# The norm of the context's tokens for its second FFN is listed ahead of the latents' mixers of the first layer

## The chip, the cores and the metric

The kernel runs on one core of a Trainium2 chip. The metric is the device time of one execution in microseconds (us), the median of three runs. The core's engines are called PE (matrix products), DVE (element-wise work on 128 partitions), ACT (activations and copies), POOL (a second element-wise engine) and SP (which issues the DMAs here); each of them works through its own list of instructions, and an instruction waits for semaphores that others raise.

## What is computed

Two layers of a diffusion backbone run over 512 latent tokens `x` and 256 context tokens `ctx`, of width 1024 each. A layer is half an FFN, four mixers side by side (convolution, RG-LRU, RWKV-7, attention) between one input projection and one output projection, and half an FFN again. In the first layer the context has its own mixers and its own second FFN; the latents' attention, RG-LRU and RWKV take states from the context. In the second layer the context only feeds the latents' mixers. Cut to what matters:

```python
def rms_norm(x): return x * rsqrt(mean(x * x, -1) + EPS)
def modulate(x, shift, scale): return rms_norm(x) * (1 + scale) + shift
def swiglu(h, w13, w2):
    gate, up = split(h @ w13, 2); return (silu(gate) * up) @ w2
for l in range(2):
    x  = x  + 0.5 * g1  * swiglu(modulate(x,  sh1,  s1),  ffn1_w13[l], ffn1_w2[l])
    xc = xc + 0.5 * g1c * swiglu(modulate(xc, sh1c, s1c), ffn1_w13[l], ffn1_w2[l])
    u, uc = modulate(x, sh2, s2) @ w_in[l], modulate(xc, sh2c, s2c) @ w_in[l]
    ya..yd, yca..ycd = conv, lru, rwkv, attention of u (with states of uc) and of uc
    x = x + g2 * concat(ya..yd) @ w_out[l]
    if l == 0:
        xc = xc + g2c * concat(yca..ycd) @ w_out[l]
        xc = xc + 0.5 * g3c * swiglu(modulate(xc, sh3c, s3c), ffn2_w13[l], ffn2_w2[l])   # its modulate is what the change lists elsewhere
    x = x + 0.5 * g3 * swiglu(modulate(x, sh3, s3), ffn2_w13[l], ffn2_w2[l])
return rms_norm(x, final_norm)
```

## The kernel before

Activations lie transposed in the core's memory: eight tiles of 128 features by 512 (or 256) tokens for `x` (or `ctx`). The numbers are float32, and a product is made of three cheaper ones: `h` and a weight are each held as a high and a low part. For a weight tile there is a load from memory (`loadw`, L483, issued on SP), a cast to the high part on ACT (`splitw`, L496, `whi`), a subtraction for the low part on DVE or POOL (L500, `wlo`), and then `gemm` (L509): 16 matmuls with `whi` and 8 with `wlo` for 128 columns of output. There are three buffers for `raw`, two for `whi` and `wlo` each, and three banks for the results that are called `pg`.

A norm (`norm`, L460 and following) has two steps. `squares` is 8 squarings on ACT (L445, tile `nsq`, two buffers) and 8 additions on POOL and DVE (L448, L450, tile `nacc`), and then it yields. The second step sums over the features with one matmul against ones on PE (`colsum`, L406, into a `pg` bank), takes the root on ACT (L415) and the reciprocal on DVE (L416), and makes 8 tiles of `h`, each by a product on DVE (L471, tile `nt`), the high part on ACT (L472) and the low part on DVE (L473); then it yields again. The norm of `x` ahead of the mixers is done in two halves of 256 tokens; the norm of `ctx` in one.

What runs when: Python lists the instructions; a scheduler then orders each engine's list ahead of time, by a model of its own in which what is listed earlier has the higher priority and what is listed later fills idle time. So the place in the listing decides the place on an engine, and on the chip each engine keeps to the order it was given. In the first layer, `Net.run` lists the mixers of the latents, `mix(0, sx, ...)`, and behind them the rest of `ff`, a chain of generators with the norm and the second FFN of the context. The scheduler takes instructions of `ff` forward into the mixers wherever an engine has nothing else to do; this is called the filler below.

`mix` for the latents is, in order: the input projections (`winproj_c`, `winproj`: matmuls L509 of `h_6104`.. `h_6111` with `w_in`, each result read by ACT at L732, L734 or L805, L815), the depthwise convolution on DVE (`taps`, L841, tile `ac`), attention's values and keys (L914, L915 `vt`, L924) and gates (a gelu at L817 to L821, tile `gy`; L819 is its ACT function), the RG-LRU (L873 and following), the RWKV scan, and the output projection.

Of the kernel before, what the change touches and what calls it, by code (L numbers as in the profile page):

```python
# [133 lines left out]
def upto(g, blocks):  # L134

    for end in g:
        blocks -= end
        yield
        if not blocks:
            return  # L140


def some(g, n):

    for _ in g:
        for _ in range(n - 1):
            next(g, None)
        yield
# [31 lines left out]
class Net:  # L180
# [1149 lines left out]
    def run(self):  # L1330
# [3 lines left out]
        with self.hidden(sx) as f:  # L1334
            self.weights("left", 4, 3, 3)
            with self.pool("aw", "right") as ap:
# [10 lines left out]
                def feed():  # L1347
                    while True:
                        next(todo, None)
                        yield  # L1350
# [3 lines left out]
                def after():  # L1354
                    yield from self.norm(f.fp, hx.hs, 0, 1, sx)

                ff = self.ffn_groups(0, "ffn1_w13", "ffn1_w2", 0, sx, f, feed(), after())
# [29 lines left out]
        with self.hidden(sc) as f:  # L1387
            late = upto(a1, 1)
            ff = chain(self.norm(f.fp, f.hs, 0, 2, sc), self.ffn_groups(0, "ffn2_w13", "ffn2_w2", 2, sc, f, late))
            self.mix(0, sx, True, None, hx.hs)  # L1390
            hp = self.hold("fh", "right")
            fx = Unit(hs=self.htiles(hp, sx))
            with self.pool("wn", "right") as wp:
                done(self.norm(wp, fx.hs, 0, 2, sx, self.pM))
            done(chain(ff, late))
            f.hs = self.htiles(f.hp, sc)
            done(self.norm(f.fp, f.hs, 1, 0, sc))
            self.ffn(1, "ffn1_w13", "ffn1_w2", 0, sc, f)
        f = fx
        with self.pool("fw") as f.fp:  # L1400
            hs = self.htiles(hp, sx)
            ff = self.ffn_groups(0, "ffn2_w13", "ffn2_w2", 2, sx, f, some(upto(a1, 1), 2), self.norm(f.fp, hs, 1, 0, sx))
# [39 lines left out]
```

## Time and profile before

| | |
|---|---|
| median of 3 runs | 3342.19 us (3340.38 to 3343.66) |
| the profiled execution | 3344.68 us, of which 3342.9 us are the span that the trace shows |
| mean granted clock of PE | 0.975 of full speed |
| busy, of the span | PE 3183.0 us (95%), DVE 2014.6 us (60%), ACT 1381.7 us (41%), POOL 962.9 us (29%) |

A row of the timeline gives the start and the length in us, the engine, the program's line and the operation, the tile written and the tiles read, and the count of like instructions that were put together; in square brackets stands how long the engine was idle just before, and whose result ended that. A windows row gives, for one stretch, each engine's busy time and its instructions, PE's granted clock as a share of full speed, and the DMA engines' busy share.

### The profile page before, as it was taken

What the parts mean: (1) busy time and instruction counts of PE and PEld (TensorE: products, weight loads), DVE (VectorE), ACT (ScalarE), POOL (GpSimd) and SP (SyncE); (2) the same over time, 40 slices, a digit from 0 to 9 for tenths busy, and PEclk for the clock granted to TensorE, in tenths of its full rate; (3) what the DMA queues carried; (4) which work ended last, traced back from release to release, by engine and by line L of the source; (5) the groups of instructions that cost most, each with busy time, mean ns of one, the idle gap of its engine ahead of it and who ended that gap; (6) DMA issues with size and microseconds to landing.
All of it is one profiled execution on the core that took longest, in us unless ns stands there. A gap on an engine that the chain in (4) does not pass through costs nothing.

```text
span 3342.9 us, 52628 instructions
## 1 busy us (share of the span) xinstructions
PE 3183.0 (95%) x20670; PEld 2578.1 (77%) x20670; DVE 2014.6 (60%) x3437; ACT 1381.7 (41%) x2362; POOL 962.9 (29%) x1205
## 2 busy tenths in 40 slices
PE   7999999999898999899999999999999889899998
PEld 3798867777776788789887778888888746688887
DVE  4555864544788656876866644543337978573335
ACT  3444553233536543545546333432225235642223
POOL 0122211441331115872222521111114266111111
PEclk9999999999999999999999999999999999999999
DMA  8656554442223344444444334233333151133232
GB/s 332 204 178 197 153 162 132 140 120 86 78 75 109 120 158 134 108 109 138 145 149 133 90 86 132 77 105 97 96 100 102 48 163 27 51 120 95 95 100 83
DMA packets 203543, 403.43 MB, mean 121 GB/s; under 512 B 97568, under 2 KB 103200, under 8 KB 203296
## 3 DMA queue, kind: packets, MB, share of 16 engines
q1 hardware_dynamic: 203296, 400.07, 39.2%
q8 instruction: 163, 2.67, 0.3%
q14 instruction: 84, 0.69, 0.1%
HBM read 392.39 MB, written 7.61 MB: 120 GB/s over the span
## 4 chain that ended last, share of the span: by engine, by line
PE 50%; DVE 9%; POOL 3%; ACT 2%; issue 2%; DMA 1%; SPq 0%; DVEq 0%; POOLq 0%; ACTq 0%
PE pg L509 41%; PE pt L509 1%; DVE ac L841 1%; PE pm L509 1%; POOL bz L1199 1%; POOL bt L1198 1%; PE pg L380 1%; DVE wlo L500 1%; DVE nacc L448 1%; DVE h L473 1%; PE pm L1242 1%; PE pm L1141 1%; DVE nt L471 0%; PE pt L954 0%; ACT whi L496 0%
## 5 line engine op out<-in xcount | busy, mean ns | idle before, releaser
L509 PE MATMUL pg<-h,whi 128*128 128x256 f32 (+1 forms) x6128 | 1214.5, 346 | 17.7 <-ACT whi L496 9.5
L509 PEld LDWEIGHTS pg<-h,whi 128*128 128x128 f32 x6128 | 979.1, 192 | 203.9 <-issue 33.7
L500 POOL TENSOR_TENSOR wlo<-raw,whi 128x1024 fp32r<-128x1024 f32 (+1 forms) x234 | 537.5, 2298 | 1923.1 <-ACT whi L496 1087.0
L496 ACT CAST whi<-raw 128x1024 fp32r<-128x1024 f32 (+1 forms) x621 | 606.7, 979 | 1067.2 <-PE pg L509 854.4
L500 DVE TENSOR_TENSOR wlo<-raw,whi 128x1024 fp32r<-128x1024 f32 (+1 forms) x387 | 450.9, 1166 | 402.2 <-PE pg L509 191.6
L509 PE MATMUL pg<-h,wlo 128*128 128x256 f32 (+1 forms) x3064 | 626.3, 343 | 2.6 <-POOL wlo L500 2.1
L509 PE MATMUL pg<-hid,whi 128*128 128x256 f32 (+1 forms) x2688 | 541.2, 338 | 14.9 <-DVE ft L558 3.9
L509 PEld LDWEIGHTS pg<-h,wlo 128*128 128x128 f32 x3064 | 490.3, 190 | 81.6 <-issue 12.0
L509 PEld LDWEIGHTS pg<-hid,whi 128*128 128x128 f32 x2688 | 420.8, 191 | 82.4 <-issue 8.3
L509 PE MATMUL pg<-hid,wlo 128*128 128x256 f32 (+1 forms) x1344 | 287.4, 333 | 1.0 <-DVE wlo L500 1.0
L528 DVE SCALAR_TENSOR_TENSOR x<-pg,msc,x 128x512 f32<-128x512 f32 (+1 forms) x232 | 154.3, 673 | 180.4 <-PE pg L509 179.4
L509 PEld LDWEIGHTS pg<-hid,wlo 128*128 128x128 f32 x1344 | 216.1, 191 | 25.5 <-DVE wlo L500 1.2
L523 DVE TENSOR_TENSOR hid<-ft,hid 128x512 fp32r<-128x512 f32 (+1 forms) x154 | 140.3, 911 | 54.8 <-ACT hid L522 54.1
L522 ACT CAST hid<-ft 128x512 fp32r<-128x512 f32 (+1 forms) x154 | 81.3, 528 | 204.0 <-DVE ft L558 203.7
L558 DVE SCALAR_TENSOR_TENSOR ft<-pg,ft 128x512 f32<-128x512 f32 (+1 forms) x152 | 86.8, 571 | 127.3 <-PE pg L509 126.8
L841 DVE SCALAR_TENSOR_TENSOR ac<-z,dw,ac 128x512 f32<-128x512 f32 (+1 forms) x180 | 142.3, 831 | 1.2
L557 DVE SCALAR_TENSOR_TENSOR ft<-ft,pg 128x512 f32<-128x512 f32 (+1 forms) x152 | 86.2, 567 | 84.5 <-ACT ft L556 84.0
L1198 POOL TENSOR_TENSOR bt<-bu,bz 32x14 f32<-32x14 f32 (+6 forms) x336 | 111.5, 332 | 22.9
L1199 POOL TENSOR_TENSOR bz<-bz,bt 32x14 f32<-32x14 f32 (+6 forms) x336 | 109.6, 326 | 23.7
L556 ACT ACTIVATE ft<-pg 128x512 f32<-128x512 f32 (+1 forms) x152 | 76.7, 504 | 79.8 <-PE pg L509 79.5
L528 DVE SCALAR_TENSOR_TENSOR ctx<-pg,msc,ctx 128x256 f32<-128x256 f32 x144 | 67.9, 480 | 44.8 <-PE pg L509 42.0
L472 ACT ACTIVATE h<-nt,mod 128x256 fp32r<-128x256 f32 x136 | 64.5, 503 | 64.4 <-DVE nt L471 64.1
(355 smaller groups left out, 3335.0 us busy)
## 6 DMA issues: line engine op xcount, KB each, us to landing
raw<-in_ffn_w_dram SPq DMA_DIRECT2D x456, 512.0 KB, 3.6
aw<-in_ada_w_dram SPq DMA_DIRECT2D x72, 512.0 KB, 5.2
raw<-in_ada_w_dram SPq DMA_DIRECT2D x72, 512.0 KB, 3.7
raw<-in_w_in_dram SPq DMA_DIRECT2D x65, 512.0 KB, 3.6
raw<-in_w_out_dram SPq DMA_DIRECT2D x56, 256.0 KB, 3.2
raw<-in_ffn_w_dram SPq DMA_DIRECT2D x40, 256.0 KB, 2.8
dl<-lq SPq DMA_DIRECT2D x48, 64.0 KB, 2.7
xt<-dz SPq DMA_DIRECT2D x48, 64.0 KB, 2.4
```

The costliest lines, as they stand in the source:

```text
L496: nc.scalar.copy(out=hi[:, 0:n], in_=raw[:, 0:n])
L500: eng.tensor_tensor(out=lo[:, 0:n], in0=raw[:, 0:n], in1=hi[:, 0:n].bitcast(F32), op=ALU.subtract)
L509: self.mm = self.nc.tensor.matmul(seg(ps[0:m, 0:N], s), W[w][:, k, c0:c0 + m], seg(hs[k][:, q, 0:N], s), start=(first and i == 0), stop=(l ...
L522: nc.scalar.copy(out=dst[:, 0, 0:N], in_=src[:, 0:N])
L523: nc.vector.tensor_tensor(out=dst[:, 1, 0:N], in0=src[:, 0:N], in1=dst[:, 0, 0:N].bitcast(F32), op=ALU.subtract)
L528: self.nc.vector.scalar_tensor_tensor(out=x, in0=seg(ps[:, 0:S.n], s), scalar=gate(m, S.i), in1=x, op0=ALU.mult, op1=ALU.add)
L556: nc.scalar.activation(out=t, in_=pg[:, 0:N], func=AF.Tanh, scale=0.5)
L557: nc.vector.scalar_tensor_tensor(out=t, in0=t, scalar=1.0, in1=pg[:, 0:N], op0=ALU.add, op1=ALU.mult)
L558: nc.vector.scalar_tensor_tensor(out=t, in0=pu[:, 0:N], scalar=0.5, in1=t, op0=ALU.mult, op1=ALU.mult)
L841: V.scalar_tensor_tensor(out=ac, in0=z, scalar=w, in1=ac, op0=ALU.mult, op1=ALU.add)
L1198: nc.gpsimd.tensor_tensor(out=tt, in0=u.u[:, I, k:k + 1].to_broadcast([32, n, m]), in1=z[:, k:k + 1, J].to_broadcast([32, n, m]), op=ALU.mult)
L1199: nc.gpsimd.tensor_tensor(out=z[:, I, J], in0=z[:, I, J], in1=tt, op=ALU.subtract)
```

## The change

Before the mixers of the latents are listed, the program now takes two steps of `ff`. These are the two steps of the context's norm for its second FFN; the FFN's own groups stay listed behind the mixers.

```diff
         with self.hidden(sc) as f:
             late = upto(a1, 1)
             ff = chain(self.norm(f.fp, f.hs, 0, 2, sc), self.ffn_groups(0, "ffn2_w13", "ffn2_w2", 2, sc, f, late))
+
+            next(ff), next(ff)
             self.mix(0, sx, True, None, hx.hs)
```

No instruction of the norm is new, and all of it stands ahead of the latents' projections in the listing. What that does to the engines' orders is seen at two places.

First PE, where the FFN before ends and the projections of `x` begin. `nacc_8341` holds the sums of squares of the second half of `x`, `h_6104` and its like are the normed `x`, `whi_8426` is the first weight tile. Of before:

```order
L509 MATMUL pg_8332<-hid_8100,wlo_8321 128x2x128
L406 MATMUL pg_8365<-nacc_8341,on 128x256
L509 MATMUL pg_8436<-h_6104,whi_8426 128x256 x2
L509 MATMUL pg_8436<-h_6105,whi_8426 128x256 x2
L509 MATMUL pg_8436<-h_6106,whi_8426 128x256 x2
```

And of the change, where `nacc_8422` holds the sums of squares of `ctx` (numbers of tiles listed behind the norm are higher by 61):

```order
L509 MATMUL pg_1444_8332<-hid_1385_8100,wlo_1442_8321 128x2x128
L406 MATMUL pg_1455_8365<-nacc_1446_8341,on_91 128x256 [waits DVE_49]
L406 MATMUL pg_1485_8446<-nacc_1476_8422,on_91 128x256 [waits DVE_49]
L509 MATMUL pg_1501_8497<-h_1067_6104,whi_1496_8487 128x256 [waits Activation_49]
L509 MATMUL pg_1501_8497<-h_1067_6104,whi_1496_8487 128x256
```

The matmul of the context's norm has moved from behind the last projection to ahead of the first one. It waits for DVE, whose order of the change has the context's additions behind all of the work on `x`:

```order
L473 SCALAR_TENSOR_TENSOR h_1074_6111<-nt_1463_8397,mod0_142,h_1074_6111 128x2x128 [waits Activation_49]
L448 TENSOR_TENSOR nacc_1476_8422<-nsq_1480_8431,nsq_1481_8433 128x256 [waits Activation_49]
L448 TENSOR_TENSOR nacc_1476_8422<-nacc_1476_8422,nsq_1482_8436 128x256 [waits Activation_49]
L450 TENSOR_TENSOR nacc_1476_8422<-nacc_1476_8422,nacc_1475_8421 128x256 [waits DVE_49,Pool_49]
L448 TENSOR_TENSOR nacc_1476_8422<-nacc_1476_8422,nsq_1483_8440 128x256 [waits DVE_49,Activation_49]
L448 TENSOR_TENSOR nacc_1476_8422<-nacc_1476_8422,nsq_1484_8443 128x256 [waits DVE_49,Activation_49]
```

On ACT the eight squarings of `ctx` stand directly behind the last L472 of `x`. So between the last tile of the normed `x` and PE's next matmul there is now this chain.

Second PE and ACT at the end of the projections. PE of before, with `pg_12531` the sums of `ctx`, `wkv` a weight of the attention, and `h_8413` the first tile of the normed `ctx`:

```order
L509 MATMUL pg_9235<-h_6111,wlo_9232 128x512
L406 MATMUL pg_12531<-nacc_12507,on 128x256
L914 MATMUL pm_9351<-wkv_9342,ckv_6097 128x256
L914 MATMUL pm_9354<-wkv_9342,ckv_6097 128x256
L914 MATMUL pm_9357<-wkv_9342,ckv_6097 128x256
L914 MATMUL pm_9360<-wkv_9342,ckv_6097 128x256
L924 MATMUL pm_9364<-ckv_6097,wkv_9342 64x512
L509 MATMUL pg_12579<-h_8413,whi_12569 128x256
```

PE of the change at the same place:

```order
L509 MATMUL pg_9296<-h_6111,wlo_9293 128x512
L509 MATMUL pg_12579<-h_8413,whi_12569 128x256 x2
...
L509 MATMUL pg_12579<-h_8420,wlo_12570 128x256
L509 MATMUL pg_12580<-h_8413,whi_12575 128x256 x2
L509 MATMUL pg_12580<-h_8414,whi_12575 128x256 x2
L509 MATMUL pg_12580<-h_8415,whi_12575 128x256 x2
L380 MATMUL pg_12636<-raw_12637,cT 32x512 x2
```

The first 24 matmuls of the context's FFN now follow the last projection, with nothing of the norm between. ACT of before there:

```order
L816 ACTIVATE gy_1591_9261<-pg_1589_9235 128x512
L415 ACT_TABLE_LOAD
L415 ACTIVATE nacc_2183_12506<-pg_2193_12531,veps_97 128x256 [waits PE_49]
L915 COPY vt_1597_9350<-pm_1598_9351 128x256 [waits PE_49]
L915 COPY vt_1597_9350<-pm_1599_9354 128x256 [waits PE_49]
L915 COPY vt_1597_9350<-pm_1600_9357 128x256 [waits PE_49]
L819 ACT_TABLE_LOAD
L819 ACTIVATE gy_1591_9261<-gy_1591_9261 128x512 [waits DVE_49]
```

ACT of the change there:

```order
L816 ACTIVATE gy_9322<-pg_9296 128x512
L496 CAST whi_12643<-raw_12641 128x1024
L819 ACTIVATE gy_9322<-gy_9322 128x512
L556 ACTIVATE ft_12629<-pg_12579 128x256
L915 COPY vt_9411<-pm_9412 128x256
```

The root and both table loads around it are gone from this place, and the third weight tile of the FFN (`whi_12643`) is cast here.

## Rows read from the trace of the kernel before

**Rows 1.** The page, busy time of each engine over the span.

```profile
PE 3183.0 (95%) x20670; PEld 2578.1 (77%) x20670; DVE 2014.6 (60%) x3437; ACT 1381.7 (41%) x2362; POOL 962.9 (29%) x1205
```

**Rows 2.** The page, the chain that ended last, by engine.

```profile
PE 50%; DVE 9%; POOL 3%; ACT 2%; issue 2%; DMA 1%; SPq 0%; DVEq 0%; POOLq 0%; ACTq 0%
```

**Rows 3.** Timeline where the projections of x begin, 888 to 903 us.

```profile
888.59 1.22 PE L406 MATMUL pg<-nacc,on 128*128 128x256 f32 x2 [4.42 <-DVE nacc L448]
889.24 6.28 PE L509 MATMUL pg<-h,whi 128*128 128x256 f32 x31
...
899.13 0.91 ACT L472 ACTIVATE h<-nt,mod 128x256 fp32r<-128x256 f32 x2 [0.95 <-DVE nt L471]
899.68 0.89 DVE L473 SCALAR_TENSOR_TENSOR h<-nt,mod,h 128x256 fp32r<-128x256 f32 x2 [0.18 <-ACT h L472]
899.95 0.71 ACT L445 ACTIVATE nsq<-ctx 128x256 f32<-128x256 f32 x2
...
900.73 0.73 POOL L448 TENSOR_TENSOR nacc<-nsq,nsq 128x256 f32<-128x256 f32 x1 [19.61 <-ACT nsq L445]
...
901.32 1.05 ACT L496 CAST whi<-raw 128x1024 fp32r<-128x1024 f32 x1 [0.66 <-PE pg L509]
...
903.16 6.70 PE L509 MATMUL pg<-h,whi 128*128 128x512 f32 x28
```

**Rows 4.** Timeline, additions of the context's squares, here and in layer two.

```profile
907.62 1.19 POOL L448 TENSOR_TENSOR nacc<-nacc,nsq 128x256 f32<-128x256 f32 x1
...
911.50 0.43 DVE L450 TENSOR_TENSOR nacc<-nacc,nacc 128x256 f32<-128x256 f32 x1
...
1697.66 0.72 ACT L445 ACTIVATE nsq<-ctx 128x256 f32<-128x256 f32 x2
...
1705.86 0.95 DVE L448 TENSOR_TENSOR nacc<-nacc,nsq 128x256 f32<-128x256 f32 x2
```

**Rows 5.** Windows, busy time of each engine, around and behind the projections' start.

```profile
888.00:894.00 6.00, 5.41 (x23) 5.24 (x24) 5.84 (x12) 2.84 (x7) 0.00 (x0) 0.50 0.00 0
...
900.00:990.00 90.00, 90.00 (x410) 71.72 (x409) 77.26 (x90) 42.77 (x62) 41.18 (x18) 1.00 0.29 89
```

**Rows 6.** Timeline, a wait of PE within the projections.

```profile
997.52 2.08 PE L435 MATMUL pm<-cst,r 128*128 128x128 f32 x8 [6.32 <-DVE r L416]
```

**Rows 7.** Timeline, end of the projections and start of the filler, 1017 to 1032 us.

```profile
1017.55 2.02 PE L509 MATMUL pg<-h,wlo 128*128 128x512 f32 x8
...
1023.09 0.63 ACT L819 ACTIVATE gy<-gy 128x512 f32<-128x512 f32 x1 [6.70 <-DVE gy L818]
1023.63 1.03 ACT L496 CAST whi<-raw 128x1024 fp32r<-128x1024 f32 x1
...
1025.04 0.60 ACT L816 ACTIVATE gy<-pg 128x512 f32<-128x512 f32 x1
1025.66 1.28 ACT L415 ACT_TABLE_LOAD   x1
...
1026.96 0.47 ACT L415 ACTIVATE nacc<-pg,veps 128x256 f32<-128x256 f32 x1
...
1027.46 1.75 DVE L416 RECIPROCAL nacc<-nacc 128x256 f32<-128x256 f32 x1 [1.08 <-ACT nacc L415]
...
1027.75 2.07 PE L914 MATMUL pm<-wkv,ckv 128*128 128x256 f32 x4 [5.31 <-ACT vt L915]
...
1032.04 0.51 PE L509 MATMUL pg<-h,whi 128*128 128x256 f32 x2 [0.72 <-ACT h L472]
```

**Rows 8.** Windows, the same columns, the filler's first stretches.

```profile
1020.00:1040.00 20.00, 11.99 (x45) 6.10 (x44) 15.87 (x32) 12.66 (x23) 1.52 (x2) 0.83 0.33 110
1040.00:1100.00 60.00, 57.38 (x370) 43.04 (x369) 49.08 (x76) 48.09 (x75) 7.11 (x3) 1.00 0.36 106
...
1310.00:1440.00 130.00, 110.81 (x1164) 97.32 (x1163) 116.73 (x244) 59.27 (x137) 105.48 (x204) 0.91 0.39 105
1400.00:1440.00 40.00, 30.07 (x373) 23.29 (x372) 37.72 (x88) 20.43 (x54) 33.46 (x70) 0.79 0.27 65
```

## Prediction

> **What bounds the kernel now.** I read the page first. PE is busy for 95% of the span, DVE for 60%, ACT for 41% [rows 1], and the chain that ended last lies half on PE and 9% on DVE, the next [rows 2]. So time is lost or won where PE stands idle or runs at half its clock, and a busy share over the whole span says nothing of a change that touches two places. The two places come from the orders: PE's matmul of the context's norm has moved from the end of the latents' projections to their beginning. I therefore read the timeline of the beginning, then of the end, and then windows to see how much idle time the stretches behind have.
>
> At the beginning PE has waited 4.42 us for the sums of squares of `x`, does that small matmul at 888.59 and starts the projections at 889.24, while DVE and ACT are still making the second half of the normed `x` [rows 3]. ACT's last L472 and DVE's last L473 of `x` end around 900, and ACT's first squarings of `ctx` start at 899.95; POOL adds them at 900.73, after it had been idle for 19.61 us [rows 3]. The reader is to see that these squarings are done this early already before the change: they fill idle time. What follows them is the new thing.
>
> **The stall at the beginning (cost).** In the new order PE may not start a projection before the matmul on `nacc_8422`, and that waits for DVE's last addition of the context's squares, which stands behind all of DVE's work on `x`. ACT's squarings stand behind the last L472 of `x`. So their start stays at 899.95. From there: two squarings take 0.71, a POOL addition 0.73 [rows 3], a DVE addition 0.43 and two of them 0.95 [rows 4]. With two buffers for `nsq`, the third squaring waits for POOL's first addition (ended 901.46), the fifth for POOL's second. That gives: third squaring to 901.9, POOL to 902.7, fifth squaring to 903.2, first DVE addition to 903.6, sixth and seventh squaring to 904.4, additions with L450 between to 905.0, eighth squaring and the last two additions to 905.9. PE's matmul then starts at about 906.0, and the first projection 0.65 us behind it, as before (889.24 less 888.59): 906.65 for 889.24.
>
> How long the first two projections take was read as well: from 889.24 to 903.16, that is 13.92 us for 96 matmuls. PE's granted clock was 0.50, its lower level of 1.2 GHz, from 888 to 894, after the idle time of 4.42 us [rows 5]. After 17 us of idle time I expect the same, so 13.92 again, and the third projection starts at 920.6 instead of 903.16: **+17.4 us**.
>
> Bounds. The lower one takes the full clock from the start: 65 matmuls took from 895.52 to 903.16, or 0.118 each, so 96 take 11.3 and the cost is 14.8. The upper one takes the squares of `ctx` in layer two, where they have other work around them: from 1697.66 to 1706.81, or 9.15 us instead of 6.0 [rows 4], hence 20.5. An addition on POOL took 1.19 instead of 0.73 when DVE was busy beside it [rows 4], which is why the chain could be slower; but in the new order DVE and POOL have nothing else to do until PE delivers a projection, so I take 17.4.
>
> Nothing hides it. From 900 to 990 PE is busy for 90.00 of 90 us [rows 5], so the projections have no slack to catch up in. The filler can't fill the wait, since all of it (the context's FFN) needs this very norm. The remaining half of the norm (reciprocal, eight times L471 to L473) lies beside the first two projections, on engines that have nothing to read from PE until those end. The cast of the third weight, at 901.32 before [rows 3], waits for PE's release of a weight buffer, which moves by the same 17. A later wait of PE, 6.32 us for a reciprocal that stands behind DVE's convolution taps [rows 6], neither goes nor grows: both sides move together.
>
> **The gain at the end of the projections.** Before, the last projection ends at 1019.4 and PE does little for 12 us: it waits 5.31 us for `vt`, and 0.72 for an `h` of the context [rows 7]. What was late is ACT: it had waited for the gelu's DVE part until 1023.09, cast a weight, read the next projection, and then loaded a table (1.28), took the root of the context's sums and only then read `vt`; the reciprocal took DVE 1.75 more, and the `h` came after that [rows 7]. In the stretch 1020 to 1040 PE is busy for 11.99 of 20 us, at a clock of 0.83; in 1040 to 1100 for 57.38 of 60 [rows 8]. Idle time is thus 8.0 and 2.6, together 10.6 us, and 11.99 at 0.83 could have been 10.0 at full clock: at most 12.6 us are to be had.
>
> With the change the 24 matmuls `pg_12579` follow the last projection at once: 24 by 0.118 is 2.8 us, to 2.8 after its end. The next 24 need `whi_12575`, cast by ACT at 1023.63 to 1024.66 behind the same gelu [rows 7]; that is 5.3 after the end, and PE idles for 2.4. The third group needs its bank read by ACT behind the second gelu, for which I count 1 us more, and small waits for `vt` and the RG-LRU's weights, another 1 us. So 10.6 idle become some 4.4, a gain of 6.2; with most of the 2.0 for the clock, **8.0 us**. Bounds: 4 (only the wait for `vt` goes, and a part of it returns as the wait for the cast) and 12.6.
>
> The rule that bears on the table loads: the Trainium skill's page "ScalarE: Activation LUTs", section "What ACT_TABLE_LOAD costs", puts a switch at 1.28 us for the load and about 1.38 for a drain. Here the load took 1.28, the activation before it had ended at 1025.64, 0.02 us ahead of it, and the one behind it started at 1026.96, again 0.02 later [rows 7], so the trace shows no drain. Were the page's figure paid, two loads fewer would free ACT for an estimated 5.3 us, not 2.6, and if PE got all of the difference the sum below would be about 6.7 instead of 9.4.
>
> **The sum.** +17.4 less 8.0 is **+9.4 us**. The profiled execution of 3344.68 us (span 3342.9) would become 3354.1; it lies 2.5 above the median of the runs, so I put the sum on the median: 3342.19 + 9.4 = **3351.6 us**, or 0.28% more. A change under 0.2%, 6.7 us, can hardly be told from none here.
>
> **The rivals.**
> 1. *The end gives back nearly all.* If the stall is at its lower bound (14.8) and the gain at its upper (12.6), 2.2 us are left: 3344.4, not told from no change. For it: ACT and DVE lose 4 to 9 us of work in the stretch where the filler starts, so later waits there may go too. Against: the wait for `whi_12575` depends on the gelu's chain on DVE, which the change leaves.
> 2. *Faster, by the RWKV stretch.* From 1310 to 1440 PE is busy for 110.81 of 130 us at a clock of 0.91, most of it missing from 1400 to 1440 (30.07 of 40, clock 0.79) [rows 8]: 19 us idle, and 10 for the clock. There the filler has run dry until the context's next norm. The new order has the filler some three weight tiles ahead by the end of the mixers. Should the dry place meet less of this stretch, up to 29 us could come back; it decides for "faster" from 16 us on (9.4 + 6.7), and 18 would give 3333. Against: in the order the context's next norm stands almost where it stood among the RWKV's steps, so the hole should move with it.
> 3. *Slower still.* The filler is used earlier and runs dry earlier: if the hole of 1400 to 1440 (10 us) grows by half and the clock falls there, some 7 us are added: 3358.6.
> That the change does nothing is ruled out by the moved matmul.
>
> **How the numbers follow.** Forecast (+4 to +16): 0.60, of which 0.08 lie under the 6.7. Rival 1: 0.20. Rival 2: 0.12. Rival 3: 0.08. So slower 0.52 + 0.08 = 0.60, same 0.08 + 0.20 = 0.28, faster 0.12. The forecast's own range runs from 17.4 less 12.6 to 20.5 less 4, that is 3347 to 3359. The range for 8 in 10 takes in rival 1 with a point or two of rival 2 below it, and most of rival 3: 3341 to 3361.
>
> **What would show it.** In the new profile PE should have an idle time of about 17 us ahead of the first projection, released by DVE's `nacc` L448, with its matmul L406 near 906 and half clock behind it; the third projection near 920.6; the wait of 6.3 for L416 still there, near 1015. At the end of the projections, near 1037, no L415 and no table load for it, 24 matmuls at once, and an idle time of some 2.4 us ended by ACT's `whi`. The window of 20 us from there should hold about 16 busy. The prediction is wrong if PE starts a projection before 900, if the end gives back more than 12.6, or if the stretch of RWKV differs by more than 5 us.

## The result, and the profile after

The changed kernel takes **3367.20 us** (median of 4 runs, 3360.15 to 3367.87) against 3341.47 us of the kernel before beside it: a ratio of **1.0070**, 95% interval 1.0058 to 1.0083. It is slower by 25.7 us where 9.4 were forecast, and lies outside the range. Its profiled execution took 3366.86 us with a span of 3364.9; the one of before lay 3.2 above its median, so the two profiles differ by 22.

The page, busy time and the chain that ended last, as in [rows 1, 2]:

```profile
PE 3186.8 (95%) x20670; PEld 2576.3 (77%) x20670; DVE 2013.6 (60%) x3437; ACT 1377.3 (41%) x2358; POOL 971.7 (29%) x1205
...
PE 54%; DVE 11%; ACT 3%; POOL 2%; issue 2%; DMA 1%; SPq 0%; DVEq 0%; ACTq 0%; POOLq 0%
```

The work is the same but for four table loads of ACT (87 instead of 91); the span holds more idle time. Timeline where the projections begin, as [rows 3] (this profile reaches the place 1.83 us earlier, so add that to compare):

```profile
898.10 0.71 ACT L445 ACTIVATE nsq<-ctx 128x256 f32<-128x256 f32 x2
898.88 0.72 POOL L448 TENSOR_TENSOR nacc<-nsq,nsq 128x256 f32<-128x256 f32 x1 [19.57 <-ACT nsq L445]
...
903.31 0.95 DVE L448 TENSOR_TENSOR nacc<-nacc,nsq 128x256 f32<-128x256 f32 x2
...
904.32 1.22 PE L406 MATMUL pg<-nacc,on 128*128 128x256 f32 x2 [16.34 <-DVE nacc L448]
...
904.98 3.98 PE L509 MATMUL pg<-h,whi 128*128 128x256 f32 x16
...
918.71 3.89 PE L509 MATMUL pg<-h,whi 128*128 128x512 f32 x16
```

PE waits 16.34 us for the last addition of the context's squares, and the third projection starts at 918.71 instead of 903.16: 15.55 later, and with the 1.83 it is 17.4. The wait within the projections is as in [rows 6]:

```profile
1013.07 2.08 PE L435 MATMUL pm<-cst,r 128*128 128x128 f32 x8 [6.32 <-DVE r L416]
```

Timeline at the end of the projections, as [rows 7]:

```profile
1034.88 2.07 PE L509 MATMUL pg<-h,whi 128*128 128x256 f32 x16
...
1036.79 1.12 PE L509 MATMUL pg<-h,wlo 128*128 128x256 f32 x8
...
1038.16 0.63 ACT L819 ACTIVATE gy<-gy 128x512 f32<-128x512 f32 x1 [6.30 <-DVE gy L818]
1038.70 1.03 ACT L496 CAST whi<-raw 128x1024 fp32r<-128x1024 f32 x1
...
1039.78 0.98 PE L509 MATMUL pg<-h,whi 128*128 128x256 f32 x6 [1.88 <-ACT whi L496]
```

The 24 matmuls of the filler follow the last projection at once, no root and no table load stands on ACT, and PE waits 1.88 us for the cast weight. The forecast's picture of both places holds. What it did not hold is seen in windows that cut both profiles at nearly the same places (the columns are those of [rows 5]; the 200 us behind the first window are alike in both and left out). Before: the 80 us behind the projections, the RWKV stretch, the rest up to the norm of `x` for its second FFN, then the second layer from its norm of `x` on (its projections, its mixers, what follows):

```profile
1019.40:1100.00 80.60, 69.97 (x415) 49.33 (x414) 65.55 (x108) 60.75 (x96) 8.93 (x5) 0.96 0.35 109
...
1300.00:1500.00 200.00, 180.81 (x1986) 161.69 (x1988) 165.43 (x337) 93.41 (x208) 156.48 (x304) 0.93 0.40 107
1500.00:1717.00 217.00, 208.07 (x1857) 196.80 (x1854) 146.03 (x254) 117.60 (x193) 52.49 (x29) 1.00 0.49 149
2546.90:2660.00 113.10, 104.00 (x542) 87.81 (x541) 101.18 (x136) 43.40 (x62) 40.61 (x16) 0.95 0.21 65
2660.00:2980.00 320.00, 288.35 (x2593) 202.28 (x2592) 237.76 (x527) 158.15 (x382) 136.59 (x320) 0.93 0.30 81
2980.00:3342.00 362.00, 347.70 (x1644) 291.53 (x1642) 157.76 (x195) 105.97 (x132) 57.07 (x27) 0.99 0.32 99
```

After, the same pieces:

```profile
1034.90:1116.40 81.50, 76.50 (x473) 55.70 (x473) 62.22 (x95) 56.86 (x86) 12.16 (x6) 1.00 0.43 137
...
1316.40:1520.00 203.60, 178.81 (x1928) 159.29 (x1928) 166.44 (x338) 91.62 (x205) 159.48 (x305) 0.91 0.40 106
1520.00:1728.40 208.40, 203.52 (x1841) 192.30 (x1841) 145.88 (x249) 113.05 (x190) 54.85 (x29) 0.99 0.50 150
2558.70:2671.90 113.20, 104.10 (x542) 87.87 (x541) 101.28 (x136) 43.37 (x62) 40.55 (x16) 0.95 0.21 65
2671.90:3002.00 330.10, 293.19 (x2593) 202.75 (x2592) 235.85 (x526) 160.30 (x384) 140.15 (x321) 0.91 0.29 78
3002.00:3364.00 362.00, 347.70 (x1644) 291.54 (x1642) 157.94 (x195) 104.17 (x130) 56.22 (x27) 0.99 0.33 99
```

PE's idle time is the length less its busy time. Behind the projections it falls from 10.6 to 5.0 us, in the RWKV stretch it grows from 19.2 to 24.8 (and the clock falls from 0.93 to 0.91), up to the norm it falls from 8.9 to 4.9. In the second layer two pieces are alike to 0.1 us, and the one between, the mixers, takes 330.1 us instead of 320.0. The edit touches nothing there. PE's longest waits in that piece, of before (total, times, longest):

```profile
PE pg L509 <- ACT whi L496: 6.4, 3, 3.5
PE pg L1089 <- ACT ta L1093: 4.7, 2, 4.5
PE pt L954 <- ACT p L961: 2.5, 3, 1.2
```

and of after:

```profile
PE pt L406 <- DVE nacc L448: 4.5, 2, 2.5
PE pg L1089 <- ACT ta L1093: 4.5, 1, 4.5
PE pc L1288 <- ACT w L1284: 3.7, 2, 3.0
PE pc L1297 <- ACT uv L1291: 3.1, 3, 1.9
```

They are other waits: the scheduler, which orders the engines ahead of time, has put the second layer's mixers into another order. DVE's rows, for one, are the same in both orders in what runs just ahead of these mixers, and differ in them.

### The profile page after: what moved, and what is told of

Its sections match the earlier page's. It is cut to its first block, busy times and chain, and to the rows that moved or that the text cites. A ratio compares the mean times of both kernels' runs of the same rounds, so it can differ in the third digit from the quotient of the medians.

```text
span 3364.9 us, 52631 instructions
## 1 busy us (share of the span) xinstructions
PE 3186.8 (95%) x20670; PEld 2576.3 (77%) x20670; DVE 2013.6 (60%) x3437; ACT 1377.3 (41%) x2358; POOL 971.7 (29%) x1205
## 4 chain that ended last, share of the span: by engine, by line
PE 54%; DVE 11%; ACT 3%; POOL 2%; issue 2%; DMA 1%; SPq 0%; DVEq 0%; ACTq 0%; POOLq 0%
PE pg L509 44%; DVE ac L841 3%; PE pt L509 1%; PE pg L380 1%; PE pm L509 1%; DVE wlo L500 1%; DVE nacc L448 1%; PE pm L1242 1%; PE pm L1141 1%; POOL bt L1198 1%; PE pt L954 1%; POOL bz L1199 1%; ACT whi L496 0%; DVE nt L471 0%; PE pc L976 0%
## 5 line engine op out<-in xcount | busy, mean ns | idle before, releaser
L509 PE MATMUL pg<-h,whi 128*128 128x256 f32 (+1 forms) x6128 | 1208.1, 345 | 8.1 <-ACT whi L496 5.4
L509 PEld LDWEIGHTS pg<-h,whi 128*128 128x128 f32 x6128 | 975.8, 191 | 192.5 <-issue 37.6
L500 DVE TENSOR_TENSOR wlo<-raw,whi 128x1024 fp32r<-128x1024 f32 (+1 forms) x387 | 458.5, 1186 | 409.6 <-PE pg L509 192.6
L509 PE MATMUL pg<-h,wlo 128*128 128x256 f32 (+1 forms) x3064 | 627.4, 344 | 2.5 <-POOL wlo L500 2.5
L509 PE MATMUL pg<-hid,whi 128*128 128x256 f32 (+1 forms) x2688 | 542.3, 338 | 20.4 <-DVE ft L558 6.3
L509 PEld LDWEIGHTS pg<-h,wlo 128*128 128x128 f32 x3064 | 490.7, 190 | 83.2 <-issue 13.3
L509 PEld LDWEIGHTS pg<-hid,whi 128*128 128x128 f32 x2688 | 421.5, 191 | 89.1 <-issue 8.6
L509 PE MATMUL pg<-hid,wlo 128*128 128x256 f32 (+1 forms) x1344 | 290.4, 334 | 1.0 <-DVE wlo L500 1.0
L509 PEld LDWEIGHTS pg<-hid,wlo 128*128 128x128 f32 x1344 | 216.7, 191 | 26.5 <-DVE wlo L500 1.2
L472 ACT ACTIVATE h<-nt,mod 128x256 fp32r<-128x256 f32 x136 | 64.6, 504 | 73.4 <-DVE nt L471 73.3
```

The source lines that it names most:

```text
L500: eng.tensor_tensor(out=lo[:, 0:n], in0=raw[:, 0:n], in1=hi[:, 0:n].bitcast(F32), op=ALU.subtract)
L509: self.mm = self.nc.tensor.matmul(seg(ps[0:m, 0:N], s), W[w][:, k, c0:c0 + m], seg(hs[k][:, q, 0:N], s), start=(first and i == 0), stop=(l ...
```

## The experiments

To compare kernels, each profile is cut at four places: the first projection of `x` (start of the L406 on `x`'s sums), the end of its last projection, and the roots L415 of two norms of `x`, which are these rows of before

```profile
1717.03 0.48 ACT L415 ACTIVATE nacc<-pm,veps 128x256 f32<-128x256 f32 x1 [0.23 <-PE pm L406]
...
2546.87 0.47 ACT L415 ACTIVATE nacc<-pg,veps 128x256 f32<-128x256 f32 x1 [0.52 <-PE pg L406]
```

and these of after.

```profile
1728.38 0.48 ACT L415 ACTIVATE nacc<-pm,veps 128x256 f32<-128x256 f32 x1 [0.21 <-PE pm L406]
...
2558.65 0.47 ACT L415 ACTIVATE nacc<-pg,veps 128x256 f32<-128x256 f32 x1 [0.63 <-PE pg L406]
```

The first cut lies between 880.5 and 888.6 us in the profiles although PE's order ahead of it is the same in all of them; that is spread between executions, and is not compared. All times in the table are us of the profiled executions; "h early" says whether the context's normed tiles are made in the projections; "order" is that of PE's instructions in the second layer from its mixers to the end: b is that of before, each other one has a letter, and lists that differ only in the few rows around a barrier or an added instruction share theirs. "Scan idle" is PE's idle time from the first to the last of the 32 updates (L1306 on DVE, tile `su`) of the state of the latents' RWKV scan, a cut at the same instructions of the scan in every kernel.

| kernel | ratio to before (95%) | h early | order | projections | to the norm of x | to layer 2's mixers | to the end | scan idle |
|---|---|---|---|---|---|---|---|---|
| before | 1 | no | b | 131.0 | 697.5 | 829.8 | 796.0 | 13.0 |
| after | 1.0070 (1.0058–1.0083) | yes | A | 148.3 | 693.3 | 830.3 | 806.2 | 19.4 |
| e1_bank | 1.0038 (1.0026–1.0050) | yes | D | 135.2 | 696.1 | 829.9 | 804.0 | 17.3 |
| e2_behind_two | 1.0042 (1.0030–1.0054) | yes | b | 143.0 | 696.9 | 830.1 | 797.9 | 18.5 |
| e3_change_barrier | 1.0080 (1.0067–1.0093) | yes | b | 148.1 | 696.8 | 821.4 | 816.0 | 20.2 |
| e4_before_barrier | 1.0059 (1.0047–1.0071) | no | E | 130.6 | 697.1 | 822.9 | 822.2 | 13.6 |
| e5_before_matmul | 1.0015 (1.0006–1.0024) | no | C | 128.3 | 700.1 | 825.5 | 808.0 | 13.1 |
| e6_change_matmul | 1.0073 (1.0057–1.0089) | yes | C | 145.8 | 701.5 | 824.4 | 810.8 | 20.1 |
| e7_sums_only | 1.0062 (1.0047–1.0077) | yes | A | 147.1 | 693.6 | 828.4 | 808.9 | 17.8 |
| e8_squares_only | 0.9997 (0.9989–1.0006) | no | b | 130.2 | 698.7 | 831.6 | 799.2 | 13.8 |
| e9_stall_alone | 1.0058 (1.0045–1.0070) | no | F | 147.1 | 696.7 | 830.1 | 805.1 | 13.3 |
| e10_behind_all | 1.0000 (0.9991–1.0009) | no | b | 131.1 | 698.1 | 832.8 | 797.8 | 13.1 |
| e11_behind_rwkv_part | 1.0054 (1.0042–1.0067) | yes | E | 133.9 | 709.0 | 830.8 | 801.2 | 18.3 |
| e12_before_two_matmuls | 0.9997 (0.9989–1.0006) | no | G | 128.6 | 702.2 | 825.6 | 798.4 | 14.3 |
| e13_before_tile | 0.9986 (0.9978–0.9995) | no | b | 128.5 | 697.8 | 825.1 | 797.3 | 15.8 |
| e14_change_tile | 1.0059 (1.0046–1.0072) | yes | A | 145.7 | 698.8 | 827.0 | 804.3 | 17.9 |
| e15_before_tile16 | 1.0000 (0.9991–1.0009) | no | b | 130.3 | 697.0 | 829.5 | 799.9 | 13.3 |

By the names that the trace shows, the rows of all four engines stand in e7 as in after, and in e8 and e10 as in before. So these three are repeats. How far profiles of one order lie apart is seen from 693.3, 693.6 and 696.8 us to the norm of `x` (after, e7 and e3, which is like after up to there), and from 796.0 to 799.9 us to the end in the kernels with order b and no barrier.

Theory 1: the missing time is the other order of the second layer's mixers, and the change's own two places cost about what the forecast says. Theory 2, the rival: all of the loss comes from what the change does in the first layer (the wait, and what it leaves behind it), whatever the order later. Theory 3, which the expectations name as well, is about the first layer alone: it loses in the RWKV stretch, since with the norm early the filler runs dry there sooner, and the wait at the beginning isn't needed for that.

**e1_bank.** The norm of the change takes its sum in another set of banks than `pg`.

```diff
-            ff = chain(self.norm(f.fp, f.hs, 0, 2, sc), self.ffn_groups(0, "ffn2_w13", "ffn2_w2", 2, sc, f, late))
+            ff = chain(self.norm(f.fp, f.hs, 0, 2, sc, self.pM), self.ffn_groups(0, "ffn2_w13", "ffn2_w2", 2, sc, f, late))
+            next(ff), next(ff)
             self.mix(0, sx, True, None, hx.hs)
```

> The change as it is, but the matmul that sums the context's squares takes its result bank from another pool (the banks called pm) instead of the three pg banks. In the order that matmul then stands within the fourth projection of x instead of ahead of the first, and the order of the second layer's mixers is nearly that of before. Theory 1 (the stall ahead of the first projection costs 17.4 us, and the other order of the second layer's mixers some 10): neither is left, the norm is still early, so the time is that of before less a few us: 3332 to 3341. Theory 2 (the second layer's loss has nothing to do with the order there; it comes with any change of the first layer): about 3347 to 3352. Theory 3 (the loss of the first layer is the filler that runs dry in the RWKV stretch, because the norm is early; the stall would have been made good): the hole from 1400 to 1440 grows here as well, 3346 to 3354.

3354.02 us. The timeline of PE has no wait for `nacc` of the context: the projections go on, and the small matmul comes within the fourth.

```profile
901.29 6.69 PE L509 MATMUL pg<-h,whi 128*128 128x512 f32 x28
...
914.83 0.59 PE L406 MATMUL pm<-nacc,on 128*128 128x256 f32 x2
...
1000.53 2.08 PE L435 MATMUL pm<-cst,r 128*128 128x128 f32 x8 [9.76 <-DVE r L416]
```

So the wait hung on the banks: with `pg`, the norm's sum has a place in the row of banks ahead of the first projection's, and with `pm` it hasn't. But 13 us remain. The wait for L416 has grown from 6.32 to 9.76, since DVE now makes the context's `h` ahead of it; the projections take 4.2 more; and order D of the second layer takes 8.0 more. Theory 1 had 3332 to 3341 and missed by 13. The scan idles for 17.3 us although the wait at the beginning is gone, as theory 3 says.

**e2_behind_two.** The two steps of the norm are listed behind the first two projections.

```diff
+        if self.early is not None:
+            self.early()
+            self.early = None
         for c in range(8):
...
+            self.early = lambda: (next(ff), next(ff))
             self.mix(0, sx, True, None, hx.hs)
```

> The two steps of the norm are listed behind the first two projections of x instead of ahead of them. PE's matmul of the norm then stands behind those 96 matmuls, and may wait some 3 us for DVE's sums; the second layer's order on DVE, ACT, POOL and SP is that of before. Theory 1: the stall is 0 to 3 us, the gain at the end of the projections stays: 3333 to 3343. Theory 2: 3348 to 3354. Theory 3: 3346 to 3354.

3354.97 us. The wait is still there, only shorter by the work ahead of it:

```profile
909.03 1.22 PE L407 MATMUL pg<-nacc,on 128*128 128x256 f32 x2 [9.59 <-DVE nacc L449]
909.69 5.55 PE L510 MATMUL pg<-h,whi 128*128 128x512 f32 x16
```

(lines are one higher here). The 16 matmuls behind it take 5.55 us and not 3.89, at a granted clock of 0.69 from 909.0 to 915.3: the clock is paid a second time. The projections take 12.0 more. The second layer has kept order b, and from the end of the projections on the pieces differ from before by -0.6, +0.3 and +1.9 us. So a wait of this kind does not by itself cost anything in layer two. The time misses the 3333 to 3343 of theory 1, whose stall of 0 to 3 us was 9.59.

**e3_change_barrier, e4_before_barrier.** A barrier of all engines ahead of the second layer's mixers, in the change and in before.

```diff
         f.hs, self.rest = hs, a1
+        self.tc.strict_bb_all_engine_barrier()
         self.mix(1, sx, True, f)
```

> The change, with a barrier over all engines ahead of the second layer's mixers. The barrier has the side effect that the order of the second layer's mixers becomes that of before, while the first layer's order is the change's. The barrier itself costs some 2 to 10 us. Theory 1: 3367 less about 10 plus the barrier: 3358 to 3368, and at most 6 us above the next run (before with the barrier). Theory 2: 3369 to 3377, and some 22 us above the next run.

> The kernel before, with the same barrier. Here it turns the order of the second layer's mixers into one that is near the change's. Theory 1: before plus about 10 plus the barrier, 3353 to 3362. Theory 2: before plus the barrier alone, 3343 to 3352.

3367.97 and 3360.36 us, 7.6 apart. The change with a barrier has order b in the second layer, and before with a barrier has E. Up to the norm of `x` they differ by 844.9 less 827.7, 17.2 us; from there on the change with the barrier is 7.7 us faster. The 7.6 lies near the 6 of theory 1 and far from the 22 of theory 2, although the first layer's loss is larger than theory 1 had it.

**e5_before_matmul, e6_change_matmul.** One unused matmul of 128 columns, with a tile of 128x8 to read it, listed ahead of the second layer's mixers in e5, and earlier, ahead of the latents' second FFN of the first layer, in e6. Both kernels then have the same order C in the second layer's mixers; it differs from A in 29 of PE's some 4600 rows there. Of e5:

```diff
+        t = self.pG()
+        self.nc.tensor.matmul(t[:, 0:128], self.ident, self.ident, start=True, stop=True)
+        q = self.small.tile([128, 8], F32, tag="nul", name=self.nm("nul"), bufs=1)
+        self.nc.vector.memset(q, 0.0)
+        self.nc.vector.tensor_tensor(out=q, in0=t[:, 0:8], in1=q, op=ALU.add)
```

> The kernel before, with one matmul of 128 columns and one addition of 8 columns put ahead of the second layer's mixers; nothing of the computation uses them. Every engine's order up to there is that of before, word for word; behind it the scheduler gives the second layer's mixers another order (call it C). Theory 1 (the order there is worth some us by itself): the first layer as before, and 3345 to 3358, all of the difference between 2660 and 2980 us. Theory 2 (the second layer's loss does not come of the order): as before, 3339 to 3344.

> The change, with the same matmul and addition, put ahead of the latents' second FFN of the first layer. The second layer's mixers then have the same order C as in the run before this one. Theory 1: the difference to that run is what the first layer loses, 10 to 15 us. Theory 2: 3365 to 3370 whatever the other run does.

3345.66 and 3368.58 us, 22.9 apart: this speaks against theory 1, by which they should have stood closer. By pieces, the first layer differs by 18.9 us (17.5 in the projections, 1.4 behind them), the piece between the layers' mixers by -1.1, and the second by 2.8; the rest, 5.1, lies ahead of the first cut. So with one order in both, little is left in layer two, as theory 1 says, but the first layer has given back all of the gain at the projections' end. e5 alone loses 12.0 us behind the last cut against before, by one unused matmul; its median shows only 3, since two pieces ahead of it are faster, the projections by 2.7 and the piece before the last by 4.3 (see e13).

**e7_sums_only, e8_squares_only.** e7 lists the squares, the sum and the root early, and the tiles of `h` late; e8 only the squares.

```diff
             rs = self.invrms(accs, bank)
+            if getattr(self, 'part', False):
+                yield
             for c in range(8):
...
+            self.part = True
+            next(ff), next(ff)
+            self.part = False
             self.mix(0, sx, True, None, hx.hs)
```

```diff
+            next(ff)
             self.mix(0, sx, True, None, hx.hs)
```

> Only the first part of the norm is listed ahead of the mixers: the squares, PE's sum over the features, the root and its reciprocal; the normed tiles h of the context are listed where the whole norm was before. PE's matmul stands ahead of the first projection as in the change, and the second layer's mixers have the change's order. Theory 1: the same stall of 17.4 us, the gain at the end of the projections partly gone since ACT and DVE make h there again, about 4 us for that; the second layer loses its 10: 3366 to 3374. Theory 3 (the first layer loses because the filler runs dry in RWKV, not by the stall): with h late the filler is no longer ahead, and the first layer is within 4 us of before: 3349 to 3356.

> Only the first of the two steps is taken early (the squares and their additions); PE's sum and all behind it are listed as before. PE's matmul stands at the end of the projections as before, and the order of the second layer's mixers is that of before. Theories 1 and 3: no stall, no early filler: 3337 to 3345. Theory 2: any change of the first layer costs the second some 10, 3349 to 3354.

e7: 3361.92 us, with the wait, order A and its 12.9 us; `h` was made early there too, in idle time. So e7 is the change a second time, and no run here has the sums early and `h` late. e8: 3341.00 us, as before: listing the squares early does nothing, since they were early already [rows 3].

**e9_stall_alone.** Before, with an unused copy of the squares, the sum and the root ahead of the projections.

```diff
+            self.invrms(self.squares(f.fp, sc, None))
             self.mix(0, sx, True, None, hx.hs)
```

> The kernel before, with a second copy of the context's squares, sum, root and reciprocal listed ahead of the mixers; nothing uses that copy, and the real norm stands where it was before. So PE has the change's wait ahead of the first projection, and nothing of the norm is early. Theory 1: the stall alone, 16 to 18 us at the beginning, and the idle time at the end of the projections stays at 10 to 11 us. If the hole in the RWKV stretch (idle 19 us before, 25 with the change) grew because the filler was early (theory 3), it stays at 19 here; if it grew because of the stall, it is 23 or more. The second layer's mixers have an order near that of the run with the other bank, which lost 7 there. In all 3358 to 3368.

3362.41 us. PE has the same wait of 16.34 us, and the projections take 16.1 more. Behind them the first layer is as before (696.7 for 697.5), with neither the gain nor the loss, and the scan idles for 13.3 us, as before: the wait alone does not make the hole there, which is theory 3 again. Order F of layer two takes 9.1 more, though it differs from b in only 69 of PE's rows and 24 of DVE's.

**e10_behind_all, e11_behind_rwkv_part.** As e2, with the call behind all projections (e10), or behind those of `winproj_c` (e11, shown).

```diff
             self.winproj_c(l, S, hs, wp, out, pr)
+            if self.early is not None:
+                self.early()
+                self.early = None
             self.winproj(l, S, hs, wp, out, pr)
```

> The norm is listed behind all input projections of x instead of ahead of them. PE's matmul of the norm then stands where it was before, the order of the second layer's mixers is that of before, and only rows of ACT and DVE around the end of the projections move. Theory 1: within 4 us of before, 3337 to 3345. Theory 2: 3349 to 3354.

> The norm is listed behind the projections of the RWKV part and ahead of the others. PE's matmul stands there, some 30 us after the context's sums are ready, so it waits for nothing; the order of the second layer's mixers is near that of the run before with the barrier, which lost 5 there. Theory 1: the first layer within 5 us of before, the second 4 to 6 more: 3343 to 3352. Theory 3 (early filler makes the hole): the first layer alone loses 5 to 10, 3351 to 3358.

e10: 3343.43 us, ratio 1.000; the order of the rows is that of before, so nothing changes. e11: 3360.91 us without any wait for the sum: the projections take 2.9 more, but the piece to the norm of `x` 11.5. Its windows in the RWKV stretch:

```profile
1311.00:1513.00 202.00, 174.62 (x1856) 152.80 (x1856) 158.85 (x325) 89.46 (x200) 151.55 (x304) 0.91 0.39 101
```

27.4 us idle, where before has 19.2. Order E takes 5.2 more behind the last cut. The time lies above what either theory 1 or theory 3 had, by 3 us for the latter. No place for this norm ahead of the projections' end pays.

**e12_before_two_matmuls.** As e5, with two of the unused matmuls, at an earlier line (`f = fx`).

> The kernel before, with two idle pairs of one matmul of 128 columns and one small addition ahead of the latents' second FFN of the first layer; nothing uses them. The order up to there is that of before, and the second layer's mixers get yet another order. Theory 1: as before up to 2660 us, and 3 to 15 us more behind it: 3344 to 3358. Theory 2: 3339 to 3344.

3342.85 us, under the 3344 to 3358 of theory 1: yet another order, G, and its last piece of 798.4 us lies within the 796.0 to 799.9 of order b. So orders differ in price, and another order need not cost anything.

**e13_before_tile, e14_change_tile, e15_before_tile16.** e5, e6 and e12 ran matmuls faster long before the added one. These runs add the tile alone, with a memset; no other instruction moves.

```diff
+        self.nc.vector.memset(self.small.tile([128, 8], F32, tag="nul", name=self.nm("nul"), bufs=1), 0.0)
         f = fx
```

> The kernel before with a tile of 128x8 float32 in the pool of small tiles and a memset of it, and nothing else; the order of all other instructions is that of before. If the faster matmuls of the runs with the added matmul (16 matmuls of 512 columns in 3.83 us where before shows 3.92) come from the tile, which shifts the places of later tiles, this run shows them too and ends at 3333 to 3339 us. If they come from the added matmul or from the order of the second layer's mixers, it ends within 2 us of before.

> The change with the same tile and memset; the order of all other instructions is that of the change. If the tile makes the matmuls faster, 3358 to 3363 us; if it does nothing, 3364 to 3369 us. By both theories the difference to the kernel before with the tile stays at 20 to 28 us: the change's stall, and the other order of the second layer's mixers.

> As the kernel before with the tile, with 128x16 in place of 128x8. If any shift of places does it, 3333 to 3339 us as with 128x8; if one shift does it and another does not, this run and the one with 128x8 differ by 4 us or more; if neither does, both are within 2 us of before.

3336.71, 3359.39 and 3341.56 us. The tile of 8 columns takes 0.14% (0.05 to 0.22%) off the kernel before, and perhaps 0.1% off the change (1.0059 for 1.0070, whose intervals overlap); a tile of 16 columns takes nothing off the kernel's time. Two groups of matmuls by form (count, busy us and mean ns), of before, of e13 and of e15:

```profile
L509 PE MATMUL pg<-h,whi 128*128 128x512 f32 x3136 | 778.3, 396 | 5.4 <-ACT whi L496 5.4
L509 PE MATMUL pg<-h,whi 128*128 128x256 f32 x2928 | 424.7, 292 | 12.4 <-ACT whi L496 4.1 <-ACT h L472 3.5 <-DVE ft L557 3.4
```

```profile
L509 PE MATMUL pg<-h,whi 128*128 128x512 f32 x3136 | 773.4, 395 | 4.1 <-ACT whi L496 4.1
L509 PE MATMUL pg<-h,whi 128*128 128x256 f32 x2928 | 418.8, 290 | 12.6 <-ACT whi L496 4.5 <-ACT h L472 3.7 <-DVE ft L557 2.2
```

```profile
L509 PE MATMUL pg<-h,whi 128*128 128x512 f32 x3136 | 778.1, 396 | 2.2 <-ACT whi L496 2.2
L509 PE MATMUL pg<-h,whi 128*128 128x256 f32 x2928 | 419.7, 290 | 12.1 <-ACT whi L496 4.1 <-ACT h L472 3.1 <-DVE ft L557 2.6
```

With this the order can be priced: e5 and e13 differ by the unused matmul and the order that it turns, and stand at 1.0015 and 0.9986, 0.29% or 9.7 us; their last piece differs by 10.7 us (808.0 and 797.3). And e14 less e13 is 22.7 us, the change's cost a second time: in the profiles 18.2 us in the first layer and 8.9 behind it, less the 5.6 by which e14's profile reaches the first cut sooner.

Taken crosswise, the last piece goes with the order and not with the early norm: with order b it takes 796.0 to 799.9 us without the early norm and 797.9 with it (e2); with order C 808.0 without (e5) and 810.8 with it (e6). PE's idle time in the scan goes with the early norm and not with that order: 13.0 to 15.8 us in the nine kernels without an early `h`, 17.3 to 20.2 in the eight with it.

## Why the prediction was wrong

**The stall: right.** +17.4 was forecast, and the third projection stands 17.4 later; the projections take 17.3 more. The chain from the first squaring to PE's matmul took 6.2 us (898.10 to 904.32) where 6.0 were worked out, and the half clock came behind it (0.50 from 904.98 to 909.00). e9 shows it by itself (16.1), and e1 that it is the banks' row.

**The wait for L416 and the end of the projections: right at their place.** The wait is 6.32 as before. Behind the projections 5.6 us of idle time are gone, and PE's clock there went from 0.96 to 1.00, which on 69.97 us of busy time is 2.8: together 8.4 against the forecast's 8.0.

By the rule on table loads of the Trainium skill's page "ScalarE: Activation LUTs", section "What ACT_TABLE_LOAD costs", two drains would have raised that gain by an estimated 2.7, to 10.7. The 8.4 of the trace lies nearer to the sum without them.

**The first step that failed is in rival 2: "in the order the context's next norm stands almost where it stood among the RWKV's steps, so the hole should move with it".** The norm does stand where it stood, behind 8 of the 32 updates of the scan in both profiles. But the hole didn't move with it, it grew, as rival 3 said, to which 0.08 were given; the forecast's sum had this stretch at nothing. The filler had less left for it: at the first update L509 has been busy for 245.1 us since the projections' end instead of 229.8, and in the first four updates it has 85 matmuls instead of 148. L509 alone there (PE busy, PEld busy, then the clock), of before,

```profile
1361.52:1398.62 37.10, 21.88 (x148) 19.02 (x148) 1.00 0.35 84
```

and of after.

```profile
1379.51:1416.14 36.63, 14.23 (x85) 11.99 (x85) 0.93 0.35 83
```

From the first update to the last, all engines, of before,

```profile
1361.52:1538.92 177.40, 164.36 (x1981) 144.78 (x1982) 132.44 (x286) 88.01 (x202) 116.42 (x234) 0.94 0.39 106
```

and of after.

```profile
1379.51:1563.37 183.86, 164.49 (x1976) 144.84 (x1977) 136.29 (x287) 84.36 (x198) 117.68 (x229) 0.92 0.40 106
```

PE is busy for the same time and the stretch is 6.5 us longer, all of it idle; that is over the 5 us that the prediction named, for this stretch, as a sign of being wrong. The whole way from the projections' end to the norm of `x` takes 2.5 us more up to the first update, 6.5 over the updates and 13.1 less behind them, where the filler done ahead is missing as work.

So of the 8 us, 4.1 are left at the norm of `x` in after, 3.9 in e7, about 0.7 in e2 and e3, and nothing in e6 and e14 against e5 and e13. Between the first cut and that norm the change costs 13.2 us in after, and 17.2 to 18.9 in the pairs e3 and e4, e5 and e6, e13 and e14; not 9.4.

**The second is the premise: "The two places come from the orders".** The orders were read around the two places and not to their ends. The listing of the second layer is unchanged, but the scheduler's choices inside its mixers are not: that piece took 10.1 us more in after's profile. Six kernels without a barrier have order b there (before, e2, e8, e10, e13, e15) and end in 796.0 to 799.9 us behind the last cut; after, e14 and e7 with order A take 804.3 to 808.9, e5 and e6 with C 808.0 and 810.8. e5 against e13 shows that the order, turned by one unused matmul, is enough, without any change in the first layer.

**The sum now.** In the profiles: 17.3 for the projections, -4.1 to the norm, +0.4 to the second layer's mixers, +10.2 to the end, -1.8 for the start, together 22.0. Theory 2 falls, since layer two costs some 8 to 10 of it by its order (10.2 in after's profile; the mean last piece of A's three lies 8.5 above that of b's six); theory 1 holds for that, and falls where it left the first layer at the forecast; theory 3 holds for what is lost there behind the projections. Three things stay open: why the scheduler turns these orders on a listing far away, which is a matter of its own model; what within an order makes it dear, since F lies near b and costs 9.1 and G lies far from it and costs nothing clear; and how much of the gain of 8 us is really kept, 4.1 in after or none in e6 and e14. Each was profiled once, e3 keeps 0.7 with the order of after, and the runs of e6 alone lie between 3353.72 and 3371.29.

No place tried for the norm beats the kernel before. The only faster kernel is e13, which isn't the change: 3336.71 us.

## What to carry to other kernels

Where a scheduler orders the engines, a change of the listing is a change of every order behind it: compare the orders to the last row before pricing anything, and price a piece that differs with both signs; here it was worth 8 to 10 us, as much as the whole forecast. A result bank that is given out in the order of listing makes an early small matmul a gate for everything behind it, so list it where its inputs are ready, or take it from other banks. And work that fills holes is only moved when it is used earlier: ask which later hole it is then missing from.

## What the runs showed of the hardware that was not expected

With a tile of 128x8 added, some 30 groups of 16 matmuls of 512 columns that take 3.89 or 3.90 us in the kernels without it, e15 with its tile of 128x16 included, take 3.82 or 3.83 in all five that have it (e5, e6, e12, e13, e14). One such group, the same matmuls of the projections in before, e13 and e15:

```profile
925.56 3.89 PE L509 MATMUL pg<-h,whi 128*128 128x512 f32 x16
```

```profile
922.97 3.82 PE L509 MATMUL pg<-h,whi 128*128 128x512 f32 x16
```

```profile
917.94 3.90 PE L509 MATMUL pg<-h,whi 128*128 128x512 f32 x16
```

The projections go with it: 128.3 to 128.6 us with that tile and 130.2 to 131.1 without, in the kernels that have before's order there. Of the totals of e13 above, 773.4 us for 512 columns lies below the 774.2 to 778.4 of all kernels without the tile; 418.8 for 256 columns does not stand out, since kernels without it lie between 417.2 and 424.7. That the places of later tiles do it is the likely cause, and wasn't tried by itself.

A barrier of all engines in the middle of the kernel costs some 7 to 15 us: e3, with order b, takes 1637.4 us behind the norm of `x`, and the six kernels with order b and no barrier 1622.4 to 1630.8.
